# Attention masks as VectorE instructions, two full-width products in place of three, and a scan whose VectorE and ScalarE work stands in program order

## The chip, the cores and the metric

The kernel runs on one core of a Trainium2 chip. The metric is the time of one execution on the device in microseconds (us). TensorE (PE in the profile; PEld is its queue of weight loads) multiplies matrices into PSUM, VectorE (DVE) and ScalarE (ACT) read PSUM and SBUF, GpSimd (POOL) works on SBUF alone, and SyncE (SP) issues the DMAs. Engines wait for one another through semaphores. Each engine takes its own instructions in the order in which the program lists them.

## The reference

One layer of a hybrid encoder over 1024 positions and 1024 channels, all in float32. Three mixers run side by side on the same projection, then they are gated, added, projected, and a gated feed-forward with a short convolution follows. What the change touches is the softmax of the two attentions and the scan:

```python
def blocked_attention(q, k, v, bias_mask):
    ...
    s = jnp.einsum('bqhd,bkhd->bhqk', q_blk, k).astype(jnp.float32) * scale
    p = jax.nn.softmax(bias_mask(i, s), axis=-1).astype(v.dtype)
    return jnp.einsum('bhqk,bkhd->bqhd', p, v)

# first attention:  allowed = (k_idx // 64) <= (q_idx // 64)
# second attention: s = s + Fq - F[k];  allowed = k_idx <= q_idx

def ssd_scan(x, dt, A, Bm, Cm):                 # 16 heads of 64, 2 groups, state 128
    ...
    y_diag = jnp.einsum('bcijg,bcijgh,bcjghp->bcighp', cb, decay, xdt)
    states = jnp.einsum('bcjgn,bcjgh,bcjghp->bcghpn', Bc, decay_to_end, xdt)
    # h[c+1] = h[c] * chunk_decay + states[c]
    y_off = jnp.einsum('bcign,bcghpn,bcigh->bcighp', Cc, h_in, jnp.exp(a_cum))
    return y_diag + y_off
```

Each attention has 8 heads. The scan's result is multiplied by a gate and normed over its 1024 channels.

## The kernel before

The positions are cut into eight tiles of 128. Products are made of a high and a low half of each operand (names ending in h and l), so that a product of two float32 matrices is three TensorE passes. The stages follow each other: norm and projections (to about 410 us), the two attentions (about 418 to 925 us), the scan (about 925 to 1120 us), the three branch projections, the output projection, and the feed-forward.

**Attention** is 64 units: 16 heads (8 of the first attention, then 8 of the second), each with four units `jp` of two query tiles. For each query tile `score_row` makes the scores, in one chunk of up to 512 keys or in two, in a PSUM tile of the ring `a_s` (3 buffers). The mask of the last 128 keys is added by TensorE too: a product of a bfloat16 unit matrix `identb` with a constant mask (`mmla` for the first attention, `mfox` for the second) into the same PSUM tile (L955). VectorE takes the row's maximum of each chunk (L957; L964 where there are two), ScalarE the exponential (L967), VectorE the reciprocal of the sum (L973), GpSimd multiplies (L974). Two units later `values` transposes the probabilities 128 by 128 on TensorE (L1021), ScalarE copies them out as the high half `pth` (L1026), VectorE makes the low half `ptl` (L1027), and `pv` multiplies by the values (L992 to L1000). The stationary operand of `pv` is `o.vv`, 128 columns wide: 64 columns of high half, 64 of low half. For the last key tile of a unit, which concerns only one of the two query tiles, three products with 64 of these columns each are made (L997 to L999). All products of a unit add up in one half of the PSUM tile `o_acc`; `done` copies its two partition halves with ScalarE into `o1` and `o2` (L1005, L1006; two buffers each), VectorE adds them (L1009) and SyncE stores the sum in `att_d` (L1010).

**The scan** is eight chunks `c`, each in three parts that run one step apart: `ssd_a` (transposes of x, the decay matrices E), `ssd_b` (products with E, products with the state, the next state, the gate and the norm's root), `ssd_c` (transposes of the result, store in `ys_d`).

**Order.** In both stages TensorE also works on the projections of gates and convolution inputs, the fill (`all_fill`, L862): 36 blocks of 48 products, of 512 columns each. `merge` interleaves the streams of a step by planned costs (`cost_s`, `cost_v`, the numbers in `yield`), and the fill gets a share by the sum of the costs. The work of the other engines is put in a list with a planned time (`later`), and issued when the planned clock has come there; `force` issues early what TensorE's next instruction needs. `tc.manual_schedule` names the engines whose instructions stay in that written order: TensorE and VectorE in attention, TensorE alone in the scan. The order on the other engines is made by a scheduler when the program is built.

Of the kernel before, what the change touches and what calls it, by code (L numbers as in the profile page):

```python
# [21 lines left out]
P = 128  # L22
# [20 lines left out]
def block_kernel(ctx: ExitStack, tc: tile.TileContext, x, positions, norm_mix_g, w_in, b_gate,  # L43
# [51 lines left out]
    identb = const([P, P], BF16, "identb")  # L95
    G.tensor_copy(identb, ident)
# [12 lines left out]
    mmla = const([P, P], BF16, "mmla")  # L109
    G.memset(mmla, 0.0)  # L110
    G.memset(mmla[0:64, 64:128], NEG)
# [826 lines left out]
    def score_row(o, i, pn):  # L938
        mask = (mmla, mfox)[o.br]
# [7 lines left out]
        for ci, (a, b) in enumerate(chunks):  # L947
# [3 lines left out]
            for i_, (q_, k_) in enumerate(o.passes):  # L951
                T.matmul(ps[:, :w], q_[:, qs], k_[:, a:a + w], start=i_ == 0,  # L952
                         stop=not last and i_ == len(o.passes) - 1)
            if last:
                T.matmul(ps[:, b - a - P:b - a], identb, mask, start=False, stop=True)  # L955
            c = len(o.passes) * w / 2400
            later(c + 0.1, lambda ps=ps, ci=ci, a=a, b=b: V.reduce_max(  # L957
# [20 lines left out]
        yield c + 0.05  # L978
# [6 lines left out]
    def values(o, jp, pn):  # L985
# [3 lines left out]
        def pv(kp, th, tl):  # L989
# [3 lines left out]
            if full:  # L993
                T.matmul(po, o.vv[:, k1, :], th[:, 256:512], start=False, stop=False)
                T.matmul(po, o.vv[:, k1, :], tl[:, 256:512], start=False, stop=False)
            else:
                T.matmul(po[0:64, 128:256], o.vv[:, k1, 0:64], th[:, 256:384], start=False, stop=False)  # L997
                T.matmul(po[0:64, 128:256], o.vv[:, k1, 64:128], th[:, 256:384], start=False, stop=False)
                T.matmul(po[0:64, 128:256], o.vv[:, k1, 0:64], tl[:, 256:384], start=False, stop=False)  # L999
# [48 lines left out]
    def cost_s(jp, n=3):  # L1048
        return sum(n * max(b - a, 256) / 2400 for i in (2 * jp, 2 * jp + 1) for a, b in row_chunks(i)) + 0.1
# [6 lines left out]
    with ExitStack() as pt__:  # L1056
# [7 lines left out]
        a_o2 = Ring(atp, [64, 256], F32, "o2", 2)  # L1064
# [33 lines left out]
    with ExitStack() as ps__:  # L1098
# [36 lines left out]

        def ssd_a(o, c):

            if c + 1 < NT:
                seg_rows(c + 1)
                load_bc(obj[c + 1], c + 1)  # L1140
            xT = pool.tile([P, D], F32, name=uid("xT"), tag="xT", bufs=1)
            for g in range(2):
                pt = psp.tile([P, 512], F32, name=uid("stp"), tag="ts", bufs=2)
                for j in range(4):
                    T.transpose(pt[:, j * P:j * P + P], o.xs[:, 4 * g + j, :], ident)
                A.activation(xT[:, 512 * g:512 * g + 512], pt, AF.Copy)
                yield 0.44
# [4 lines left out]
            V.tensor_mul(o.xdt, xv, hb(dt, c))  # L1152
            o.xdd = pool.tile([P, 16, 64], F32, name=uid("xdd"), tag="xdd", bufs=1)
            V.tensor_mul(o.xdd, xv, hb(dend, c))
            o.y = pool.tile([P, 16, 64], F32, name=uid("y"), tag="y", bufs=3)
            V.tensor_mul(o.y, xv, Db.unsqueeze(2).to_broadcast([P, 16, 64]))
            o.E = []
            o.bT = pool.tile([P, 2, P], F32, name=uid("bT"), tag="bT")
            for g in range(2):
                hs = slice(8 * g, 8 * g + 8)  # L1160
                pcb = psp.tile([P, 512], F32, name=uid("pcb"), tag="seg", bufs=2)
                T.matmul(pcb[:, 0:P], o.bc[:, g, :], o.bc[:, 2 + g, :], start=True, stop=True)
                cbm = pool.tile([P, P], F32, name=uid("cbm"), tag="cbm")
                T.transpose(pcb[:, P:2 * P], o.bc[:, g, :], ident)
                V.tensor_mul(cbm, pcb[:, 0:P], tri)
                A.activation(o.bT[:, g, :], pcb[:, P:2 * P], AF.Copy)
                yield 0.33
                for q in range(2):
                    pse = psp.tile([P, 512], F32, name=uid("pse"), tag="seg", bufs=2)
# [5 lines left out]
                    A.activation(E, pse.rearrange("p (h i) -> p h i", h=4), AF.Relu, scale=-1.0)  # L1175
                    A.activation(E, E, AF.Exp, scale=-1.0)
                    V.tensor_mul(E, E, cbm.unsqueeze(1).to_broadcast([P, 4, P]))
# [3 lines left out]
        def ssd_b(o, c, prev):  # L1181

            zt, _ = f_t4.get()
            SY.dma_start(zt, z_d[c * P:c * P + P, :])
            for g in range(2):
                hs = slice(8 * g, 8 * g + 8)
                py = psp.tile([P, 8, 64], F32, name=uid("py"), tag="py", bufs=2)
                for q in range(2):
                    for hh in range(4):
# [4 lines left out]
                V.tensor_add(o.y[:, hs, :], o.y[:, hs, :], py)  # L1194
                yield 0.88
                if prev is not None:
                    po = psp.tile([P, 512], F32, name=uid("pof"), tag="ts", bufs=2)
                    T.matmul(po, o.bc[:, 2 + g, :], prev.hst[:, hs, :], start=True, stop=True)
                    tmp = pool.tile([P, 8, 64], F32, name=uid("yo"), tag="yo", bufs=1)
                    V.tensor_mul(tmp, po.rearrange("p (h d) -> p h d", d=64), hb(ea, c, hs))  # L1200
                    V.tensor_add(o.y[:, hs, :], o.y[:, hs, :], tmp)
                    yield 0.86
            if c + 1 < NT:
                o.hst = pool.tile([P, 16, 64], F32, name=uid("hst"), tag="hst")
                for g in range(2):
                    hs = slice(8 * g, 8 * g + 8)
                    ps_ = psp.tile([P, 512], F32, name=uid("pst"), tag="ts", bufs=2)
                    T.matmul(ps_, o.bT[:, g, :], o.xdd[:, hs, :], start=True, stop=True)
                    psv = ps_.rearrange("p (h d) -> p h d", d=64)
                    if prev is None:  # L1210
                        V.tensor_copy(o.hst[:, hs, :], psv)
                    else:
                        V.tensor_mul(o.hst[:, hs, :], prev.hst[:, hs, :], hb(cdec, c, hs))
                        V.tensor_add(o.hst[:, hs, :], o.hst[:, hs, :], psv)
                    yield 0.86
            yf = o.y.rearrange("p h d -> p (h d)")
            V.scalar_tensor_tensor(out=yf, in0=yf, scalar=0.5, in1=zt, op0=ALU.mult, op1=ALU.mult)
            o.yT = pool.tile([P, 8, P], F32, name=uid("yT"), tag="yT", bufs=1)
            ss = pool.tile([P, 1], F32, name=uid("yss"), tag="yss")
            A.activation(o.yT.rearrange("p j s -> p (j s)"), yf, AF.Square, accum_out=ss)  # L1220
# [552 lines left out]
```

## Time and the profile before

| what | value |
|---|---|
| time of three runs | 2058.81, 2062.83, 2064.87 us, median 2062.83 us |
| the profiled execution | 2061.22 us; its span (first to last instruction) 2059.5 us |
| busy: PE, DVE, ACT, POOL | 98%, 67%, 46%, 30% of the span |
| mean granted clock of TensorE | 0.993 of full speed |
| attention, 418 to 925 us | DVE about 70% busy, ACT about 60% |
| scan, 925 to 1120 us | DVE about 70% busy, ACT about 50% |

In the timeline a row is one instruction, or several equal ones that follow each other (x3): when it started, how long it took, engine, line and operation, the tile written and the tiles read by the program's names (qk, pth, ptl, o, s, mm), then partitions and columns, and in brackets how long the engine had been idle and who ended that. The ends of matmuls are modelled, so the distance from one start to the next, the pitch, says what an instruction cost TensorE. Groups of instructions have a row with the count, the busy time, the mean duration of one in ns, and the idle time ahead of them with what ended it.

### The profile page before, as it was taken

How to read it: one execution, taken by the hardware profiler on the slowest of the kernel's cores; microseconds unless marked ns; L12 is line 12 of the kernel's file. 1: busy time of each engine (PE TensorE's matmuls, PEld its weight loads, DVE VectorE, ACT ScalarE, POOL GpSimd, SP SyncE). 2: the span in 40 equal slices, each digit the busy share in tenths (PEclk: the TensorE clock that was granted, in tenths of full speed). 3: DMA queues.
4: the chain of work that ended last, by engine and by line, in shares of the span. 5: the costliest groups of instructions: out<-in, count | busy, mean ns of one | idle time of the engine just before them, and what ended most of it. 6: DMA issues, size and time to landing. Idle time of an engine off the chain costs nothing.

```text
span 2059.5 us, 28796 instructions
## 1 busy us (share of the span) xinstructions
PE 2009.7 (98%) x10233; PEld 1685.1 (82%) x10233; DVE 1388.7 (67%) x2498; ACT 940.5 (46%) x1722; POOL 611.0 (30%) x604
## 2 busy tenths in 40 slices
PE   7999899999999999999999999999899999999999
PEld 7899678888888888888778888888688888878887
DVE  7678479366667766755774455567987787775655
ACT  5555323156556666555553222223544454444432
POOL 4345233222222222210000040001654445412655
PEclk9999999999999999999999999999999999999999
DMA  5158767655344455324432664431322322329665
GB/s 168 45 169 263 256 221 243 197 155 142 109 123 112 133 134 133 101 83 146 139 121 95 230 215 145 156 130 52 92 82 72 102 72 73 101 94 350 216 230 195
DMA packets 274792, 303.60 MB, mean 147 GB/s; under 512 B 18860, under 2 KB 206520, under 8 KB 274648
## 3 DMA queue, kind: packets, MB, share of 16 engines
q1 hardware_dynamic: 274648, 301.76, 46.7%
q8 instruction: 81, 1.33, 0.3%
q14 instruction: 63, 0.52, 0.1%
HBM read 209.03 MB, written 92.67 MB: 146 GB/s over the span
## 4 chain that ended last, share of the span: by engine, by line
PE 81%; DVE 9%; DMA 4%; ACT 2%; issue 2%; POOL 1%; SPq 1%; ACTq 0%; DVEq 0%; POOLq 0%
PE mm L862 19%; PE ybr L163 8%; PE dn L1720 8%; PE ua L1388 5%; PE ud L1388 5%; PE uc L1388 5%; PE fx L163 4%; PE wo L1434 4%; PE s L952 4%; PE tp L1021 3%; PE ub L1388 2%; PE fxv L163 2%; PE q L163 1%; PE py L1190 1%; PE kv L163 1%
## 5 line engine op out<-in xcount | busy, mean ns | idle before, releaser
L862 PE MATMUL mm<-hnh,wh 128*128 128x512 f32 x576 | 247.3, 429 | 0.0
L862 PE MATMUL mm<-hnh,wl 128*128 128x512 f32 x576 | 226.6, 393 | 0.0
L862 PE MATMUL mm<-hnl,wh 128*128 128x512 f32 x576 | 225.2, 391 | 0.0
L974 POOL TENSOR_SCALAR pm<-pm,rs 128x128 f32<-128x128 f32 (+7 forms) x128 | 107.9, 845 | 347.9 <-DVE rs L973 313.8
L1720 PE MATMUL dn<-dr,dr 128*128 128x512 f32 x592 | 182.1, 389 | 0.0
L1027 DVE TENSOR_TENSOR ptl<-tp,pth 128x512 fp32r<-128x512 f32 (+1 forms) x160 | 101.3, 633 | 83.0 <-ACT pth L1026 81.9
L957 DVE TENSOR_REDUCE nmx<-s 128x1 f32<-128x128 f32 (+2 forms) x192 | 105.7, 551 | 57.4 <-PE s L955 45.7
L967 ACT ACTIVATE pm<-s,nmx 128x128 f32<-128x128 f32 (+2 forms) x192 | 109.6, 575 | 55.6 <-DVE nmx L964 38.1
L1720 PEld LDWEIGHTS dn<-dr,dr 128*128 128x128 f32 x592 | 111.1, 188 | 23.0
L862 PEld LDWEIGHTS mm<-hnh,wl 128*128 128x128 f32 x576 | 108.1, 188 | 24.9
L862 PEld LDWEIGHTS mm<-hnh,wh 128*128 128x128 f32 x576 | 108.8, 189 | 17.9 <-issue 4.1
L862 PEld LDWEIGHTS mm<-hnl,wh 128*128 128x128 f32 x576 | 109.0, 189 | 17.6 <-issue 3.1
L1026 ACT ACTIVATE pth<-tp 128x512 fp32r<-128x512 f32 (+1 forms) x160 | 88.2, 551 | 70.1 <-PE tp L1021 69.3
L952 PE MATMUL s<-qk,qk 96*128 96x384 f32 (+5 forms) x480 | 117.8, 350 | 0.9 <-ACT pm L967 0.9
L1720 PE MATMUL dn<-dr 128*128 128x512 f32 x296 | 115.3, 389 | 0.4 <-DVE dY L1737 0.4
L1299 POOL TENSOR_TENSOR mg<-mg,gl 128x512 f32<-128x512 f32 x16 | 24.9, 1559 | 299.1 <-DVE gl L1296 297.6
L139 DVE TENSOR_TENSOR dr<-dr,dr 128x1024 fp32r<-128x1024 f32 x52 | 72.2, 1388 | 55.6 <-ACT dr L138 53.2
L163 PE MATMUL fx<-w5h,hnh 128*128 128x512 f32 x256 | 103.2, 403 | 2.1 <-ACT w5h L138 2.1
L163 PE MATMUL fx<-w5l,hnh 128*128 128x512 f32 x256 | 101.4, 396 | 1.4 <-DVE w5l L139 1.4
L163 PE MATMUL fx<-w5h,hnl 128*128 128x512 f32 x256 | 101.1, 395 | 0.0
L163 PE MATMUL ybr<-al,wh 128*128 128x512 f32 x256 | 99.2, 389 | 0.0
L163 PE MATMUL ybr<-ah,wl 128*128 128x512 f32 x256 | 98.3, 389 | 0.0
(492 smaller groups left out, 5698.3 us busy)
## 6 DMA issues: line engine op xcount, KB each, us to landing
dr<-act_d SPq DMA_DIRECT2D x99, 256.0 KB
wr<-in_ffn_w_up_dram SPq DMA_DIRECT2D x47, 512.0 KB
wr<-in_w_in_dram SPq DMA_DIRECT2D x36, 512.0 KB
g_d<-t SPq DMA_DIRECT2D x24, 512.0 KB
gl<-g_d SPq DMA_DIRECT2D x24, 512.0 KB
ws<-in_ffn_w_down_dram SPq DMA_DIRECT2D x22, 512.0 KB
wsum_d<-ws SPq DMA_DIRECT2D x22, 512.0 KB
act_d<-fa SPq DMA_DIRECT2D x22, 512.0 KB
```

The lines of the kernel that those rows point to most:

```text
L139: return i, le.tensor_sub(l, src, f32(h))
L163: T.matmul(ps, a(k), b(k), start=(i == 0), stop=(i == n - 1))
L862: T.matmul(ps, a[:, k, :], b[half][:, k, :], start=(k == 0 and i == 0), stop=(k == NK - 1 and i == 2))
L952: T.matmul(ps[:, :w], q_[:, qs], k_[:, a:a + w], start=i_ == 0, stop=not last and i_ == len(o.passes) - 1)
L957: later(c + 0.1, lambda ps=ps, ci=ci, a=a, b=b: V.reduce_max(nmx[:, ci:ci + 1], ps[:, :b - a], axis=AX, negate=True))
L967: pss[ci][1][0] = later(c + 0.9 + 0.1 * ci, lambda ci=ci, a=a, b=b: A.activation(p_[:, a:b], pss[ci][0][:, :b - a], AF.Exp, bias=nb, accum ...
L974: G.tensor_scalar(p_[:, 0:n * P], p_[:, 0:n * P], rs[:, 3:4], 0.0, op0=ALU.mult, op1=ALU.add)
L1026: later(c + 0.05, lambda th=th, pt=pt, off=off: A.activation(th[:, :off], pt[:, :off], AF.Copy))
L1027: pl[0] = later(c + 0.6, lambda th=th, tl=tl, pt=pt, off=off: V.tensor_sub(tl[:, :off], pt[:, :off], f32(th[:, :off])))
L1388: T.matmul(ps, a, b, start=first and n == 0, stop=n == 11, skip_group_check=not first)
L1434: T.matmul(p, a, b, start=k == 0 and i == 0, stop=k == NK - 1 and i == 2)
L1720: T.matmul(ps[m], a[:, ts_], b[:, 512:], start=first_ and j == 0 and q == 0, stop=j == NFH - 1 and q == 2, skip_group_check=not first_)
```

## The change

The TensorE products that added the masks are gone, with the constants `identb` and `mmla`. In their place VectorE writes the last 64 keys of the first 64 queries with the mask's value (`memset`, first attention), or adds `mfox` to the last 128 keys (`tensor_add`, second attention), ahead of the row's maximum. In `pv` the three products with 64 columns become two with all 128 (the high half of the probabilities, then the low half; the second adds a term of low times low). `o2` has six buffers. Two planned costs lose the mask's share. In the scan VectorE and ScalarE keep program order as well; their instructions get planned times by `later`, PSUM tiles come from rings (`s_ts`, `s_seg`, `s_py`, two buffers each as before), and `xdd`, `yT`, `yo` and `cbm` have twice the buffers.

```diff
-    identb = const([P, P], BF16, "identb")
-    G.tensor_copy(identb, ident)
...
-    mmla = const([P, P], BF16, "mmla")
...
     def score_row(o, i, pn):
...
                 T.matmul(ps[:, :w], q_[:, qs], k_[:, a:a + w], start=i_ == 0,
-                         stop=not last and i_ == len(o.passes) - 1)
-            if last:
-                T.matmul(ps[:, b - a - P:b - a], identb, mask, start=False, stop=True)
+                         stop=i_ == len(o.passes) - 1)
             c = len(o.passes) * w / 2400
-            later(c + 0.1, lambda ps=ps, ci=ci, a=a, b=b: V.reduce_max(
+            if last and o.br == 0:
+                later(c + 0.1, lambda ps=ps, e=b - a: V.memset(ps[0:64, e - 64:e], NEG))
+            elif last:
+                later(c + 0.1, lambda d=ps[:, b - a - P:b - a]: V.tensor_add(d, d, mfox))
+            later(c + 0.101, lambda ps=ps, ci=ci, a=a, b=b: V.reduce_max(
...
-        yield c + 0.05
+        yield c
...
-                T.matmul(po[0:64, 128:256], o.vv[:, k1, 0:64], th[:, 256:384], start=False, stop=False)
-                T.matmul(po[0:64, 128:256], o.vv[:, k1, 64:128], th[:, 256:384], start=False, stop=False)
-                T.matmul(po[0:64, 128:256], o.vv[:, k1, 0:64], tl[:, 256:384], start=False, stop=False)
+                T.matmul(po[:, 128:256], o.vv[:, k1, :], th[:, 256:384], start=False, stop=False)
+                T.matmul(po[:, 128:256], o.vv[:, k1, :], tl[:, 256:384], start=False, stop=False)
...
-        return sum(n * max(b - a, 256) / 2400 for i in (2 * jp, 2 * jp + 1) for a, b in row_chunks(i)) + 0.1
+        return sum(n * max(b - a, 256) / 2400 for i in (2 * jp, 2 * jp + 1) for a, b in row_chunks(i))
...
-        a_o2 = Ring(atp, [64, 256], F32, "o2", 2)
+        a_o2 = Ring(atp, [64, 256], F32, "o2", 6)
...
         def ssd_a(o, c):
...
-            V.tensor_mul(o.xdt, xv, hb(dt, c))
...
+            o.rdt = later(1.3, lambda: V.tensor_mul(o.xdt, xv, hb(dt, c)))
+            later(2.6, lambda: V.tensor_mul(o.y, xv, Db.unsqueeze(2).to_broadcast([P, 16, 64])))
+            o.rdd = xT_read[0] = later(3.9, lambda: V.tensor_mul(o.xdd, xv, hb(dend, c)))
...
         def ssd_b(o, c, prev):
...
-            A.activation(o.yT.rearrange("p j s -> p (j s)"), yf, AF.Square, accum_out=ss)
...
+            later(3.1, lambda: A.activation(o.yT.rearrange("p j s -> p (j s)"), yf, AF.Square, accum_out=ss))
+            later(4.3, root)
+            o.ry = later(6.3, lambda: A.activation(yf, yf, AF.Copy, scale=r))
...
-        with tc.manual_schedule(engines={mybir.EngineType.PE}):
+        with tc.manual_schedule(engines={mybir.EngineType.PE, mybir.EngineType.DVE, mybir.EngineType.Activation}):
```

The order on TensorE, at the seam between the second and the third unit of a head of the first attention. The rows are in program order: line, operation, tile written and tiles read, columns. Before (s: scores, o: the values' sum, tp: transposes, mm: fill):

```order
L952 MATMUL s_5744<-qk_1143_5285,qk_1146_5288 128x256
L955 LDWEIGHTS identb
L955 MATMUL s_5744<-mmla,identb 128x128
L992 MATMUL o<-pth_5648,vv_5189 128x256
L997 MATMUL o<-pth_5648,vv_5189 64x128
L998 MATMUL o<-pth_5648,vv_5189 64x128
L999 MATMUL o<-ptl_5649,vv_5189 64x128
L1000 MATMUL o<-ptl_5649,vv_5189 128x256
L1021 MATMUL tp_5760<-ident,pm_5508 128x128
L1021 MATMUL tp_5760<-ident,pm_5538 128x128 x2
L862 MATMUL mm_5766<-hnh_124,wh_5345 128x512
```

Of the fill six products (L862) follow here, and then the third unit's first L992. In the changed program, at the same seam:

```order
L946 MATMUL s_5734<-qk_1151_5278,qk_1154_5281 128x256
L988 MATMUL o<-pth_5639,vv_5183 128x256
L993 MATMUL o<-pth_5639,vv_5183 128x128
L994 MATMUL o<-ptl_5640,vv_5183 128x128
L995 MATMUL o<-ptl_5640,vv_5183 128x256
L1016 MATMUL tp_5749<-ident,pm_5501 128x128
L1016 MATMUL tp_5749<-ident,pm_5528 128x128 x2
L988 MATMUL o<-pth_5691,vv_5183 128x256
```

The mask's pair of rows is gone, three narrow products are two wide ones, and here the fill has moved to another place, so that only three transposes stand between the second unit's last product and the third's first. Over the whole stage eight of the 63 seams had only three transposes before, and nine have now; the fill has 29 products fewer in attention and 30 more behind the scan.

On VectorE, at the same row of the second attention, before (nmx: maxima, ptl: low half):

```order
L957 TENSOR_REDUCE nmx_8204<-s_8206 128x1
L1027 TENSOR_TENSOR ptl_8215<-tp_8210,pth_8214 128x384
L957 TENSOR_REDUCE nmx_8204<-s_8225 128x1
L964 TENSOR_TENSOR nmx_8204<-nmx_8204 128x1
L957 TENSOR_REDUCE nmx_8231<-s_8233 128x1
```

and in the changed program:

```order
L953 TENSOR_REDUCE nmx_8142<-s_8144 128x1
L1022 TENSOR_TENSOR ptl_8153<-tp_8148,pth_8152 128x384
L952 TENSOR_TENSOR s_8169<-s_8169,mfox 128x128
L953 TENSOR_REDUCE nmx_8142<-s_8169 128x1
L960 TENSOR_TENSOR nmx_8142<-nmx_8142 128x1
L953 TENSOR_REDUCE nmx_8184<-s_8186 128x1
```

One instruction has come in ahead of the last maximum of each row.

On VectorE in the scan, from the root of one chunk's norm to the first mask product of the next chunk's decay (cbm), before (yr: root, xdt, y, xdd: products with x, wl: fill, py: PSUM of ssd_b):

```order
L155 SCALAR_TENSOR_TENSOR yr_3959_11930<-rs_t_11936,yr_3959_11930 128x1
L1152 TENSOR_TENSOR xdt_12004<-xT_11950,dt 128x1024
L1156 TENSOR_TENSOR y_12008<-xT_11950,Db 128x1024
L151 SCALAR_TENSOR_TENSOR rs_t_11939<-yr_3959_11930,rs_v_11934 128x1
L155 SCALAR_TENSOR_TENSOR yr_3959_11930<-rs_t_11939,yr_3959_11930 128x1
L151 SCALAR_TENSOR_TENSOR rs_t_11942<-yr_3959_11930,rs_v_11934 128x1
L155 SCALAR_TENSOR_TENSOR yr_3959_11930<-rs_t_11942,yr_3959_11930 128x1
L1194 TENSOR_TENSOR y_11798<-y_11798,py_11984 128x512
L811 TENSOR_TENSOR wl_12025<-wr_12022,wh_12024 128x1024
L1165 TENSOR_TENSOR cbm_12013<-pcb_12011,tri 128x128
```

and in the changed program:

```order
L146 SCALAR_TENSOR_TENSOR rs_t_11880<-yr_4199_11814,rs_v_11872 128x1
L150 SCALAR_TENSOR_TENSOR yr_4199_11814<-rs_t_11880,yr_4199_11814 128x1
L1154 TENSOR_TENSOR xdt_11857<-xT_11819,dt 128x1024
L1155 TENSOR_TENSOR y_11859<-xT_11819,Db 128x1024
L1156 TENSOR_TENSOR xdd_11858<-xT_11819,dend 128x1024
L806 TENSOR_TENSOR wl_11838<-wr_11835,wh_11837 128x1024
L1200 TENSOR_TENSOR y_11657<-y_11657,py_11886 128x512
L1165 TENSOR_TENSOR cbm_11909<-seg_11907,tri 128x128
```

The root is no longer spread between other work: it stands in one piece, and xdd, which stood behind the state's sums, has moved ahead of wl.

More of the change, by code (lines that the diff above doesn't have):

```diff
@@ L1134, in hb @@
             return t[:, c, hs].unsqueeze(2).to_broadcast([P, hs.stop - hs.start, 64])
+        s_ts, s_seg, s_py = (Ring(psp, [P, 512], F32, n, 2) for n in ("ts", "seg", "py"))
+        xT_read = [None]
         def ssd_a(o, c):
@@ L1215, in ssd_b @@
+                        pl[0] = later(1.0, lambda hs=hs, psv=psv: V.tensor_add(
+                            o.hst[:, hs, :], o.hst[:, hs, :], psv))
+                    o.rh.append(pl[0])
                     yield 0.86
             yf = o.y.rearrange("p h d -> p (h d)")
-            V.scalar_tensor_tensor(out=yf, in0=yf, scalar=0.5, in1=zt, op0=ALU.mult, op1=ALU.mult)
-            o.yT = pool.tile([P, 8, P], F32, name=uid("yT"), tag="yT", bufs=1)
+            o.yT = pool.tile([P, 8, P], F32, name=uid("yT"), tag="yT")
@@ L1227, in ssd_c @@
+            zl[0] = later(1.8, lambda: V.scalar_tensor_tensor(out=yf, in0=yf, scalar=0.5, in1=zt,
+                                                              op0=ALU.mult, op1=ALU.mult))
+            later(3.1, lambda: A.activation(o.yT.rearrange("p j s -> p (j s)"), yf, AF.Square, accum_out=ss))
+            later(4.3, root)
+            o.ry = later(6.3, lambda: A.activation(yf, yf, AF.Copy, scale=r))
         def ssd_c(o, c):
+            force(o.ry)
             yf = o.y.rearrange("p h d -> p (h d)")
@@ L1230, in ssd_c @@
             for g in range(2):
[L1231 removed]
+                pt, pl = s_ts.get()
                 for j in range(4):
                     T.transpose(pt[:, j * P:j * P + P], yf[:, (4 * g + j) * P:(4 * g + j + 1) * P], ident)
[L1234 removed]
+                pl[0] = later(0.54, lambda g=g, pt=pt: A.activation(
+                    o.yT[:, 4 * g:4 * g + 4, :], pt.rearrange("p (j s) -> p j s", j=4), AF.Copy))
@@ L1235, in ssd_c @@
+                if g == 1:
+                    o.out = later(1.2, lambda: SY.dma_start(
+                        ys_d[:, :, c * P:c * P + P].rearrange("j p s -> p j s"), o.yT))
                 yield 0.44
-            SY.dma_start(ys_d[:, :, c * P:c * P + P].rearrange("j p s -> p j s"), o.yT)
-        with tc.manual_schedule(engines={mybir.EngineType.PE}):
+        with tc.manual_schedule(engines={mybir.EngineType.PE, mybir.EngineType.DVE, mybir.EngineType.Activation}):
             obj = {c: Head() for c in range(NT)}
@@ L1257, in block_kernel @@
                     break
+            force(obj[NT - 1].out)
     mix.close()
```

77 lines of the change are left out of this document (41 added, 36 removed).

## The prediction

> **What bounds the kernel now.** First the page's top and its chain that ended last.
>
> ```profile
> span 2059.5 us, 28796 instructions
> PE 81%; DVE 9%; DMA 4%; ACT 2%; issue 2%; POOL 1%; SPq 1%; ACTq 0%; DVEq 0%; POOLq 0%
> ```
>
> Four fifths of the chain are TensorE. Then the view of busy time by windows, for the stages that change: two windows of attention (PE, PEld, DVE, ACT, POOL busy us and instructions, granted clock, DMA share, GB/s), one of the scan.
>
> ```profile
> 600.00:700.00 100.00, 98.79 (x601) 84.03 (x600) 69.07 (x158) 61.27 (x156) 25.38 (x29) 1.00 0.48 130
> 700.00:800.00 100.00, 99.38 (x604) 84.13 (x603) 73.75 (x165) 64.47 (x158) 24.85 (x29) 1.00 0.49 129
> 950.00:1050.00 100.00, 99.39 (x531) 79.53 (x531) 71.83 (x133) 51.53 (x90) 0.00 (x0) 1.00 0.42 126
> ```
>
> TensorE is busy for 99 us of 100 at full clock, VectorE for about 70. Busy need not mean needed, so I read who TensorE waits for, in the view of waits over the whole run (us in total, times, longest):
>
> ```profile
> PE o L992 <- ACT o L1006: 8.2, 11, 1.5
> PE s L952 <- ACT pm L967: 0.9, 2, 0.6
> PE stp L1145 <- DVE rs_v L147: 0.4, 1, 0.4
> ```
>
> In attention it waits for the copy of the values' sum, and almost never for VectorE's part of the softmax; in the scan it waits 0.4 us in all. So in both stages **a TensorE instruction saved is time saved**, and a faster order in the scan has nothing to give. A change to VectorE counts only where it becomes late for TensorE.
>
> **Term 1, the 128 mask products.** TensorE's timeline, by pitch: a mask with a product of the values behind it, and the same products without a mask ahead.
>
> ```profile
> 560.06 0.23 PE L955 MATMUL s<-mmla,identb 128*128 128x128 bf16 x1
> 560.10 0.36 PE L992 MATMUL o<-pth,vv 128*128 128x256 f32 x1
> 560.30 0.22 PE L997 MATMUL o<-pth,vv 128*64 128x128 f32 x1
> ...
> 565.28 0.28 PE L992 MATMUL o<-pth,vv 128*128 128x256 f32 x1
> 565.40 0.22 PE L997 MATMUL o<-pth,vv 128*64 128x128 f32 x1
> ```
>
> The mask has a pitch of 0.04 us, and L992 behind it one of 0.20, against 0.12 without. So this mask costs 0.04 + 0.08 = 0.12 us, though its own pitch looks like nothing. Behind other masks stand transposes:
>
> ```profile
> 573.85 0.23 PE L955 MATMUL s<-mmla,identb 128*128 128x128 bf16 x1
> 573.92 0.60 PE L1021 MATMUL tp<-ident,pm 128*128 128x128 f32 x4
> 574.28 0.48 PE L862 MATMUL mm<-hnh,wh 128*128 128x512 f32 x1
> ...
> 568.86 0.60 PE L1021 MATMUL tp<-ident,pm 128*128 128x128 f32 x4
> 569.21 0.47 PE L862 MATMUL mm<-hnh,wh 128*128 128x512 f32 x1
> ```
>
> Here the mask costs 0.07, and the four transposes 0.36 instead of 0.35: 0.08 in all. In the order of instructions before, 84 masks have a product behind them and 44 have transposes: 84 x 0.12 + 44 x 0.08 = **13.6 us** saved.
>
> **Term 2, three narrow products become two wide ones.** A pitch of 0.06 for each of L997 to L999 would promise 64 x 0.06 = 3.8 us. But the last product behind them is not free:
>
> ```profile
> 565.29 0.14 PEld L997 LDWEIGHTS o<-pth,vv 128*64 128x64 f32 x1
> ...
> 565.52 0.19 PEld L1000 LDWEIGHTS o<-ptl,vv 128*128 128x128 f32 x1
> ...
> 560.48 0.33 PE L1000 MATMUL o<-ptl,vv 128*128 128x256 f32 x1
> 560.65 0.39 PE L862 MATMUL mm<-hnh,wh 128*128 128x512 f32 x1
> 560.88 0.40 PE L862 MATMUL mm<-hnl,wh 128*128 128x512 f32 x1
> ...
> 568.62 0.29 PE L995 MATMUL o<-ptl,vv 128*128 128x256 f32 x1
> 568.74 0.28 PE L1000 MATMUL o<-ptl,vv 128*128 128x256 f32 x1
> ```
>
> L1000 behind the narrow products has a pitch of 0.17, while behind L995 it has 0.12 (568.74 to 568.86, quoted above). The load of 128 columns takes 0.19, that of 64 columns 0.14: 64 columns more are 0.05 more, so 128 columns need about 0.11 of the load path. Under a narrow product of 0.06 that load doesn't hide, and 0.05 is left over. Products of few columns under full loads show the same bound:
>
> ```profile
> 1036.43 1.89 PE L1190 MATMUL py<-xdt,E 128*128 128x64 f32 x16
> 1038.16 0.44 PE L1162 MATMUL pcb<-bc 128*128 128x128 f32 x2
> ```
>
> Sixteen in 1.73 us are 0.11 each. Now the two wide products: each streams 128 columns (0.06) while the next full load (0.11) runs, so each has a pitch of 0.11. Before: 0.12 + 3 x 0.06 + 0.17 = 0.47. Changed: 0.12 + 2 x 0.11 + 0.12 = 0.46. I take 64 x 0.01 = **0.6 us** saved; the ends are 3.8 saved (both wide ones at 0.06, the one behind them still at 0.17) and 2.6 lost (0.11 each, with L1000 staying at 0.17: 0.51, 64 x 0.04).
>
> [...]
>
> **Term 3, six output copies.** Most waits for L1006 look like this one: a unit ends, three transposes, and the next unit's first product finds the sum not yet copied out.
>
> ```profile
> 571.47 0.34 PE L1000 MATMUL o<-ptl,vv 128*128 128x256 f32 x1
> 571.65 0.49 PE L1021 MATMUL tp<-ident,pm 128*128 128x128 f32 x3
> 572.74 0.39 PE L992 MATMUL o<-pth,vv 128*128 128x256 f32 x1 [0.60 <-ACT o L1006]
> ...
> 857.11 0.38 ACT L1006 ACTIVATE o<-o 64x256 f32<-64x256 f32 x1 [2.59 <-DMA att_d<-o]
> ACT o L1006 <- DMA att_d<-o: 4.6, 3, 2.6
> ```
>
> From 571.65, three transposes should have ended 0.24 later (0.35 for four above, less 0.11), at 571.89: 0.85 us lost. This has nothing to do with `o2`; it belongs to seams with three transposes alone, eight before and nine now: **0.9 us lost**. What six buffers remove is ScalarE's wait for the store, 4.6 us in three places. The longest, 2.6 us, held TensorE for up to 1.5 (its longest wait, above). I take **3 us** saved, between 1.5 and 4.6.
>
> **Term 4, VectorE's new work in attention.** 64 times a `memset` of 64 x 64 and 64 times an addition of 128 x 128 in PSUM. The second isn't in the trace; nearest are the products with `tri` from PSUM, and for the first the one larger `memset` on VectorE:
>
> ```profile
> L1165 DVE TENSOR_TENSOR cbm<-pcb,tri 128x128 f32<-128x128 f32 x16 | 4.5, 283 | 1.1 <-PE pcb L1164 1.1
> L651 DVE MEMSET neg<- x1: 165/165/165, 283.5 to 283.5; 8x128 f32 x1
> ```
>
> At 0.28 and at most 0.17 us, VectorE gets 18 us more in the second attention (about 240 us long: from some 72% busy to 80%) and 11 in the first. It isn't the bound, so the question is whether a row's chain gets late. TensorE may fill a score buffer again when ScalarE has read the chunk three before it. A typical one of the second attention:
>
> ```profile
> 714.19 0.58 ACT L967 ACTIVATE pm<-s,nmx 128x384 f32<-128x384 f32 x1 [0.18 <-DVE rs L972]
> ...
> 715.49 0.51 PE L952 MATMUL s<-qk,qk 128*128 128x384 f32 x2
> ```
>
> The buffer is free at 714.77, and wanted at 715.49: 0.72 us to spare. Of the 189 such distances five are under 0.2 us, four from 0.37 to 0.48, and the rest 0.66 or more. A chain longer by 0.28 makes TensorE wait where less was to spare, about 1 us in all, if a queue forms once or twice. I take **1 us** lost, from 0 to 6 (25 tight buffers late by 0.25 each).
>
> **Term 5, the scan in program order.** 0.4 us of wait is all there is to gain. To lose, VectorE must be late for the decay products, which reuse PSUM behind `cbm`.
>
> ```profile
> 1027.10 1.22 DVE L1217 SCALAR_TENSOR_TENSOR y<-y,t 128x1024 f32<-128x1024 f32 x1
> 1031.37 1.06 ACT L1220 ACTIVATE yT<-y 128x1024 f32<-128x1024 f32 x1 [1.58 <-DMA ys_d<-yT]
> 1032.56 0.15 DVE L1222 TENSOR_SCALAR yv<-yss 128x1 f32<-128x1 f32 x1 [1.99 <-ACT yT L1220]
> L1177 DVE TENSOR_TENSOR E<-E,cbm 128x512 f32<-128x512 f32 x32 | 22.0, 687 | 14.0 <-ACT E L1176 14.0
> ```
>
> In the new order VectorE has, from the state's last sum to `cbm`: the sum and an E (0.69 each), the gate (1.22), the wait for the square (1.06 and a read, 1.2), the root (ten small ones of 0.15 or a little more, 1.7), xdt, y, xdd and wl (1.22 each, as wide as the gate), one PSUM sum (0.69), `cbm` (0.28): 11.4 us. TensorE meanwhile has 30 fill products (0.23 each by the rows of L862 above, 6.9), three groups of four L1190 (0.86 each, 2.6), eight transposes (0.9), and pof, pst, pcb and two decay products, some 2.5: 12.9 us. VectorE is 1.5 us ahead, so **0**, from 0.4 gained to 8 lost (1 us in each chunk). Two buffers for yT also take away the wait of 1.58 for the store, which cost TensorE nothing.
>
> The fill's 29 products that leave attention come back behind the scan, where TensorE is the bound too: 0.
>
> **Sum.** 13.6 + 0.6 - 0.9 + 3 - 1 = 15.3 us saved. The profiled execution took 2061.22 us, 1.7 more than its span: 2045.9, and its like against the median of 2062.83, which is 1.6 above it, 2047.5. I say **2046 us**.
>
> **Rivals.**
> - *The mask's replacement is late.* For it: each row's chain grows by up to 0.28 us on an engine that stands at 70%. Against: 0.66 us or more to spare in 180 of 189 places. Price 6 us at the tight buffers: 2052.
> - *The scan stalls, and the kernel is slower.* The root now stands in one piece and waits for ScalarE's square with xdt, xdd, wl and `cbm` queued behind it; `cbm` is waited for by ScalarE's copy, and that by TensorE. It decides once the square comes over 1.5 us later than I count; for a kernel slower than before, each of eight chunks must lose 2 us and more, so the square be 3.5 us late: 2046 + 8 x 2.7 = 2068. For it: the wait of 1.99 above. Against: part of it was the store's. [...] No run so far shows this order.
> - *The wide products are cheap.* If they had the pitch of 0.06, 3.2 us more are saved: 2043. For it: that is what L997 to L999 show. Against: the 0.11 of L1190.
> - *Masks cost their own pitch only.* If the longer product behind a mask had another cause, 128 x 0.05 = 6.4 us are saved in place of 13.6: 2053. Against: 0.20 and 0.12 for the same L992.
>
> **How the numbers follow.** Forecast 62%, with 2041 to 2051 for its own; late masks 14%; scan 6%; wide products 10%; masks for their own pitch 8%. The range goes from 2039 (all upper ends of terms 2 and 3 together: 2046 - 3.2 - 1.6, and 2 for the spread of runs) to 2056 (late masks, with half of what the scan can lose). Runs differ by about 0.3%, which is what can be told from no change: 6.2 us, so faster means under 2056.6. The forecast and the wide products lie under it (72%), own pitch mostly (6 of 8), late masks half (7 of 14): 85% faster; within 0.3% 11%; slower 4%, from the scan.
>
> **What would show it.** The first value product (L992 before) at a pitch of 0.12 wherever scores stand ahead; the two wide products at 0.11, and the one behind at 0.12; no ScalarE wait for att_d; nine waits of 0.85 for L1001; waits of scores for exponentials of about 2 us in all; in the scan under 1 us of TensorE waits. A wait of TensorE for ScalarE's copy beside `cbm`, chunk after chunk, would make me wrong, and so would scores that wait in each unit of the second attention.

## The result and the profile after

The changed kernel takes 2048.31 us in the median of five runs (2043.96 to 2050.93), the kernel before 2062.82 beside it (2058.25 to 2064.87): a ratio of 0.9939, with a 95% interval from 0.9924 to 0.9955, or 14.5 us less by the medians, 12.6 by the ratio, 9.3 to 15.7 by the interval. The profiled execution took 2043.96 us. Its page has this span and this chain:

```profile
span 2042.2 us, 28558 instructions
PE 84%; DVE 9%; DMA 2%; ACT 2%; issue 2%; POOL 1%; SPq 1%; ACTq 0%; DVEq 0%; POOLq 0%
```

and its view of waits these rows for TensorE in attention and in the scan (us in total, times, longest):

```profile
PE o L988 <- ACT o L1001: 7.3, 11, 1.2
PE tp L1016 <- POOL pm L970: 0.9, 1, 0.9
PE tp L1016 <- DVE ptl L1022: 0.9, 2, 0.7
PE seg L1171 <- ACT bT L1166: 0.6, 1, 0.6
PE s L946 <- ACT pm L963: 0.4, 2, 0.2
```

The scan waits once, for ScalarE's copy beside `cbm`. In attention the waits for the output copy are as many as before (11), with 7.3 us in place of 8.2, and transposes now wait too.

Spans don't say where the time went, so I measure two stretches by TensorE's timeline, each without its fill (0.231 us a product). **Attention** goes from the first product of the scores to the scan's first transposition: 253.2 us before (511.0 less 1116 products), 244.0 after (494.9 less 1086). **The scan** goes from there to near the end of the first branch projection behind it: 253.1 and 251.6. So the change is worth 9.2 + 1.5 = 10.7 us in what it touches. The other 6.6 of the two profiled executions lie ahead of attention (4.8) and far behind the scan (1.8), in code that is the same. The view by windows shows why, ahead of attention; the kernel before first:

```profile
80.00:100.00 20.00, 16.64 (x87) 15.61 (x85) 12.20 (x44) 9.54 (x33) 2.12 (x10) 0.83 0.37 115
280.00:300.00 20.00, 17.77 (x80) 14.54 (x79) 16.79 (x50) 6.63 (x13) 5.10 (x4) 0.91 0.60 169
```

and the changed kernel:

```profile
80.00:100.00 20.00, 15.34 (x96) 14.28 (x96) 13.36 (x47) 10.11 (x34) 2.10 (x10) 1.00 0.38 115
280.00:300.00 20.00, 20.00 (x97) 16.58 (x96) 18.08 (x57) 6.88 (x11) 5.12 (x4) 1.00 0.73 217
```

The number behind POOL's busy time is the granted clock: 0.83 and 0.91 in one, 1.00 in the other. The clock differs between executions of one kernel too: the means of the changed kernel's five runs go from 0.992 to 0.996. Runs of the kernel before, 61 of them in the comparisons below, go from 2055.75 to 2067.32. Single differences under some 4 us are therefore read from the stretches, not from the times.

TensorE's pitches behind scores, where a mask stood before, in the changed kernel's timeline:

```profile
555.73 0.86 PE L946 MATMUL s<-qk,qk 96*128 96x512 f32 x3
556.43 0.28 PE L988 MATMUL o<-pth,vv 128*128 128x256 f32 x1
556.55 0.22 PE L993 MATMUL o<-pth,vv 128*128 128x128 f32 x1
556.61 0.28 PE L994 MATMUL o<-ptl,vv 128*128 128x128 f32 x1
556.73 0.33 PE L995 MATMUL o<-ptl,vv 128*128 128x256 f32 x1
556.89 0.52 PE L946 MATMUL s<-qk,qk 96*128 96x256 f32 x3
```

L988 has 0.12, as forecast; the wide products have 0.06 and 0.12, the one behind them 0.16. Together 0.46, as forecast, though otherwise shared out.

Now a place that came out worse. The first score product of the seventh query tile's second chunk waits for the exponential of the sixth tile's first chunk, which frees its buffer. ScalarE there in the kernel before, and TensorE:

```profile
461.63 0.58 ACT L967 ACTIVATE pm<-s,nmx 128x384 f32<-128x384 f32 x1 [2.10 <-DVE nmx L964]
462.20 0.57 ACT L967 ACTIVATE pm<-s,nmx 128x384 f32<-128x384 f32 x1
462.76 0.59 ACT L1026 ACTIVATE pth<-tp 128x512 fp32r<-128x512 f32 x1
...
462.93 0.39 PE L862 MATMUL mm<-hnh,wl 128*128 128x512 f32 x1
463.16 0.69 PE L952 MATMUL s<-qk,qk 96*128 96x384 f32 x3
463.69 0.23 PE L955 MATMUL s<-mmla,identb 128*128 128x128 bf16 x1
```

and in the changed kernel, with VectorE's minimum on which the exponential rests:

```profile
457.36 0.16 DVE L960 TENSOR_TENSOR nmx<-nmx 128x1 f32<-128x1 f32 x1
...
457.77 0.60 ACT L1021 ACTIVATE pth<-tp 128x512 fp32r<-128x512 f32 x1 [2.13 <-PE tp L1016]
458.26 0.58 ACT L963 ACTIVATE pm<-s,nmx 128x384 f32<-128x384 f32 x1
458.82 0.58 ACT L963 ACTIVATE pm<-s,nmx 128x384 f32<-128x384 f32 x1
...
458.67 0.40 PE L857 MATMUL mm<-hnh,wl 128*128 128x512 f32 x1
458.98 0.80 PE L946 MATMUL s<-qk,qk 96*128 96x384 f32 x3
459.62 0.28 PE L988 MATMUL o<-pth,vv 128*128 128x256 f32 x1
```

The minimum is there at 457.52, but ScalarE's next instruction is now the copy `pth`, which starts at 457.77, and the exponential comes at 458.26. TensorE's pitches show the rest: the last fill product takes 0.31 in place of 0.23, the three score products 0.64 in place of 0.53. That is 0.19 us, without a wait in the rows of TensorE's matmuls, since the modelled end of the last fill product (458.67 + 0.40 = 459.07) lies behind the start of the scores (458.98). The queue of weight loads does show one, of 0.34 us:

```profile
458.98 0.47 PEld L946 LDWEIGHTS s<-qk,qk 96*128 96x128 f32 x3 [0.34 <-ACT pm L963]
```

In ScalarE's program order `pth` stands ahead of this exponential in 16 heads of 16; before it stood there in 3. Before, those three heads and no others showed the longer pitches; now all do.

By pitch (what each instruction's distance to the next exceeds that of its kind where nothing is waited for), TensorE loses 18.5 us in attention now, 13.4 before: 10.1 ahead of the values' products (11.3 before), 5.5 at scores (2.0), 2.8 at transposes (none).

### The profile page after: what moved, and what is told of

It is laid out like the page before. It is cut to its first block, busy times and chain, and to the rows that moved or that the text cites. A ratio compares the mean times of both kernels' runs of the same rounds, so it can differ in the third digit from the quotient of the medians.

```text
span 2042.2 us, 28558 instructions
## 1 busy us (share of the span) xinstructions
PE 1991.4 (98%) x10041; PEld 1678.7 (82%) x10041; DVE 1410.3 (69%) x2626; ACT 944.5 (46%) x1722; POOL 617.3 (30%) x601
## 4 chain that ended last, share of the span: by engine, by line
PE 84%; DVE 9%; DMA 2%; ACT 2%; issue 2%; POOL 1%; SPq 1%; ACTq 0%; DVEq 0%; POOLq 0%
PE mm L857 18%; PE dn L1743 10%; PE ybr L158 9%; PE fx L158 6%; PE ua L1411 5%; PE uc L1411 5%; PE ud L1411 5%; PE wo L1457 4%; PE s L946 4%; PE tp L1016 3%; PE ub L1411 3%; PE fxv L158 1%; PE py L1196 1%; PE kv L158 1%; PE q L158 1%
## 5 line engine op out<-in xcount | busy, mean ns | idle before, releaser
L970 POOL TENSOR_SCALAR pm<-pm,rs 128x128 f32<-128x128 f32 (+7 forms) x128 | 113.1, 886 | 327.7 <-DVE rs L969 199.9
L963 ACT ACTIVATE pm<-s,nmx 128x128 f32<-128x128 f32 (+2 forms) x192 | 109.8, 578 | 37.3 <-DVE nmx L960 24.4
```

The costliest lines, as they stand in the source:

```text
L963: pss[ci][1][0] = later(c + 0.9 + 0.1 * ci, lambda ci=ci, a=a, b=b: A.activation(p_[:, a:b], pss[ci][0][:, :b - a], AF.Exp, bias=nb, accum ...
L970: G.tensor_scalar(p_[:, 0:n * P], p_[:, 0:n * P], rs[:, 3:4], 0.0, op0=ALU.mult, op1=ALU.add)
```

## The experiments

All runs in one table. Time is the median with the interval of the ratio to the kernel before (a median of 2060.8 to 2061.6 in each of the three sets of runs, and of 2062.8 beside the changed kernel); the stretches are as above; waits are TensorE's in attention by pitch.

| kernel | time, us | ratio's interval | attention | waits | scan |
|---|---|---|---|---|---|
| before | 2060.8 to 2061.6 | | 253.2 | 13.4 | 253.1 |
| changed | 2048.3 | 0.9924 to 0.9955 | 244.0 | 18.5 | 251.6 |
| masks only | 2060.7 | 0.9990 to 1.0017 | 260.1 | 34.0 | 252.3 |
| no mask | 2044.5 | 0.9900 to 0.9936 | 238.8 | 13.8 | 251.6 |
| ScalarE's order | 2053.7 | 0.9956 to 0.9980 | 249.6 | 23.8 | 251.7 |
| seams | 2046.5 | 0.9914 to 0.9959 | 244.6 | 18.8 | 251.6 |
| two o2 | 2060.5 | 0.9979 to 1.0005 | 255.2 | 29.3 | 251.7 |
| scan only | 2060.4 | 0.9980 to 1.0008 | 256.3 | 16.6 | 252.5 |
| seams, fill from behind | 2046.4 | 0.9899 to 0.9951 | 237.2 | 11.7 | 255.7 |
| more fill | 2050.8 | 0.9930 to 0.9968 | 242.6 | 17.3 | 256.4 |
| six o2 only | 2055.8 | 0.9962 to 0.9988 | 251.6 | 11.8 | 252.9 |
| seams, half and half | 2041.6 | 0.9898 to 0.9930 | 240.8 | 15.2 | 251.8 |
| mask twice | 2055.6 | 0.9960 to 0.9987 | 252.1 | 26.2 | 252.0 |
| narrow | 2046.4 (one run) | | 243.3 | 17.6 | 251.6 |

Some of these traces have stretches in which TensorE was granted half its clock. How long they are follows from the mean clock of windows around them: 4.00 us at 0.57 in two o2 (from 846 us) are 3.4 us at half and the rest at full clock; 2.70 at 0.79, 2.00 at 0.50 and 2.00 at 0.93 in masks only (from 726.3 us) are 3.4 as well; the 6.8 us in ScalarE's order below are twice that. A stretch of 3.4 us is so worth up to 1.7 us. The columns include them. I count, in attention, three in masks only, two in ScalarE's order, one each in seams, two o2, more fill and mask twice, and in the scan's stretch one in more fill; the windows are shown for two o2, for ScalarE's order and for one of masks only, not for the others. The kernel before and the changed one have none there: their clock is 1.00 in each window of 50 us from 450 to 1150 us.

**Masks only**, on the kernel before:

```diff
-                T.matmul(ps[:, b - a - P:b - a], identb, mask, start=False, stop=True)
+            if last and o.br == 0:
+                later(c + 0.1, lambda ps=ps, e=b - a: V.memset(ps[0:64, e - 64:e], NEG))
+            elif last:
+                later(c + 0.1, lambda d=ps[:, b - a - P:b - a]: V.tensor_add(d, d, mfox))
```

> The kernel before with the masks on VectorE alone (and the planned costs that go with them): three narrow value products, two o2 buffers and the old scan stay. Theory A (as forecast: the 128 products are worth 13.6 us and VectorE's work costs 1): about 12.6 us under the kernel before, 2050. Theory B (ScalarE's order: in this program, as in the changed one, the copy pth stands ahead of the exponential of the sixth query tile's first chunk in 16 of 16 heads, in the kernel before in 3; the scores that reuse its buffer wait 0.1 to 0.2 us in each head, and a few single waits come with it, 5 us in all): about 8.5 us under, 2054, with 16 scores of a pitch 0.1 too long.

Neither: nothing is gained. TensorE's work fell by the 12.4 us of the masks in attention (228.3 to 215.9 without waits and fill), but its waits rose by 20.6. The views of waits of this kernel, of TensorE and of ScalarE:

```profile
PE o L993 <- ACT o L1007: 17.4, 14, 4.1
ACT o L1007 <- DMA att_d<-o: 16.4, 7, 3.8
```

The largest part is the output copy, and behind it the store: by pitch some 10 of the 20.6 us. Another 5 are by my count the three stretches at half the clock, which follow waits of 2.1, 2.1 and 4.1 us for that copy (the clock is shown for the first alone), and some 6 stand at scores and transposes, as in the changed kernel. That made the next theory, the one of the pair (masks and buffers bring a gain only together), and the run with two o2 buffers.

**No mask**, on the changed kernel:

```diff
-            if last and o.br == 0:
-                later(c + 0.1, lambda ps=ps, e=b - a: V.memset(ps[0:64, e - 64:e], NEG))
-            elif last:
-                later(c + 0.1, lambda d=ps[:, b - a - P:b - a]: V.tensor_add(d, d, mfox))
```

> The changed kernel without any mask, on TensorE or on VectorE: the scores of forbidden keys stay in, nothing else is left out. In its program pth stands ahead of that exponential in 2 of 16 heads, so the two theories agree here on a gain: if VectorE's masks with all that follows cost 5 us, 2043; if they cost the 1 us of the forecast, 2047. The scores' extra pitch of 0.1 in each head goes by both.

Attention is 5.2 us shorter than in the changed kernel: this is what the masks on VectorE cost, five times the forecast. Waits at scores fall from 5.5 to 2.1, at transposes from 2.8 to 1.1. The two heads with `pth` ahead are the only ones in which the longer pitches are left.

**ScalarE's order**, on the changed kernel:

```diff
-        with tc.manual_schedule(engines={mybir.EngineType.PE, mybir.EngineType.DVE}):
+        with tc.manual_schedule(engines={mybir.EngineType.PE, mybir.EngineType.DVE, mybir.EngineType.Activation}):
```

> The changed kernel with ScalarE in program order in attention too; VectorE's masks stay as they are. pth then stands ahead of the sixth tile's first exponential in 0 of 16 heads (between its two exponentials in 7). Theory A' (VectorE's own time, 0.11 to 0.29 us more in the chain, makes the scores late): the extra pitches stay, 2048. Theory B (ScalarE's order): they go, 16 x 0.19 = 3 us less, 2045. Against both: copies of the fill in program order may stand in the way of other exponentials, then it gets slower than 2048 and new waits show.

Slower by 5, and still the place in question tells the theories apart. ScalarE and TensorE there:

```profile
459.22 0.58 ACT L963 ACTIVATE pm<-s,nmx 128x384 f32<-128x384 f32 x1 [2.04 <-DVE nmx L960]
459.80 0.57 ACT L963 ACTIVATE pm<-s,nmx 128x384 f32<-128x384 f32 x1
460.35 0.59 ACT L1021 ACTIVATE pth<-tp 128x512 fp32r<-128x512 f32 x1
...
460.15 0.39 PE L857 MATMUL mm<-hnh,wl 128*128 128x512 f32 x1
460.38 0.69 PE L946 MATMUL s<-qk,qk 96*128 96x384 f32 x3
460.91 0.28 PE L988 MATMUL o<-pth,vv 128*128 128x256 f32 x1
```

0.23 and 0.53 again, with VectorE's mask still in the chain; so in all eight heads of the first attention, and in six of the second. The regular 0.19 us (3.0 in 16 heads) is ScalarE's order. What it lost stands elsewhere: program order makes copies stand behind exponentials whose maximum isn't there yet. The worst place, ScalarE and then TensorE:

```profile
836.07 0.47 ACT L963 ACTIVATE pm<-s,nmx 128x256 f32<-128x256 f32 x1 [2.14 <-DVE nmx L953]
837.17 0.38 ACT L1000 ACTIVATE o<-o 64x256 f32<-64x256 f32 x1
...
838.01 0.58 PE L988 MATMUL o<-pth,vv 128*128 128x256 f32 x1 [3.42 <-ACT o L1001]
```

TensorE's clock is halved from 836.3 to 843.1, and the 5.1 us of this behind the wait cost another 2.5. Both ends are worked out from the view by windows (granted clock third from the end), with half or full clock in each window:

```profile
834.00:838.00 4.00, 0.55 (x3) 0.31 (x3) 2.69 (x6) 1.89 (x6) 1.56 (x3) 0.79 0.95 177
838.00:840.00 2.00, 1.99 (x8) 1.90 (x9) 0.65 (x2) 0.85 (x2) 0.00 (x0) 0.50 0.39 119
840.00:843.00 3.00, 3.00 (x10) 2.50 (x9) 2.64 (x7) 1.16 (x3) 0.03 (x1) 0.50 0.33 85
843.00:846.00 3.00, 3.00 (x20) 2.66 (x19) 1.09 (x2) 1.00 (x2) 0.85 (x1) 0.98 0.50 195
```

So this one place accounts for most of the 5.6 us that attention is longer.

**Seams**, on the changed kernel (`o_at` is the planned time of the last unit's end):

```diff
         if kp == 0:
             force(o_last[jp % 2])
+            if clk[0] - o_at[0] < 1.6:
+                owed[0] -= advance(fill) or 0.0
```

> The changed kernel with six products of the fill put ahead of a unit's first product of the values wherever less than 1.6 us are planned since the last unit's end. The eleven waits for the output copy, 7.3 us by the view of waits and 10 us by pitch, should go: 8 to 10 us less, 2039. If the waits are a debt that TensorE pays elsewhere (fill spent here is missing in another place, where scores then wait), the gain is under 4 us.

The waits for the output copy go from 10.1 to 0.1 by pitch, and the scores' rise from 5.5 to 14.5: a debt, and with the stretch at half the clock that I count behind a score's wait of 1.6 us (the clock there is not shown) it is paid in full (18.5 us of waits before, 18.8 now).

**Two o2 buffers**, on the changed kernel:

```diff
-        a_o2 = Ring(atp, [64, 256], F32, "o2", 6)
+        a_o2 = Ring(atp, [64, 256], F32, "o2", 2)
```

> The changed kernel with two o2 buffers, as before the change. By the forecast, six buffers are worth 3 us (1.5 to 4.6): 2051, 2053 at most. By the theory that came out of masks alone (where ScalarE waited 16.4 us for the stores and TensorE 17.4 us for ScalarE's output copies, so that nothing was left of the masks' 13.6 us): the buffers are worth 9 to 13 us in this kernel, 2058 to 2061, with seven or so waits of ScalarE for att_d, and TensorE's waits for the output copy at 15 to 18 us in place of 7.3.

As by the theory of the pair: 12 us by the times, 11.2 by the stretch of attention. The view of waits, for TensorE and ScalarE:

```profile
PE o L988 <- ACT o L1001: 16.7, 14, 3.8
ACT o L1001 <- DMA att_d<-o: 16.0, 8, 3.5
```

and SyncE's queue in the timeline, ahead of the longest of these waits:

```profile
834.58 0.99 SPq L919 DMA_DIRECT2D qk<-fk_h  x2
835.62 0.46 SPq L919 DMA_DIRECT2D qk<-fk_l  x1
836.18 0.55 SPq L1005 DMA_DIRECT2D att_d<-o  x1
836.78 1.23 SPq L919 DMA_DIRECT2D qk<-fq_h  x2
838.05 0.51 SPq L919 DMA_DIRECT2D qk<-fq_l  x1
838.65 0.40 SPq L802 DMA_DIRECT2D wr<-in_w_in_dram  x1
840.21 5.20 SPq L1005 DMA_DIRECT2D att_d<-o  x1
```

The six loads of the next head and a weight block go out first; the store behind them, which else takes 0.45 us to issue (the median of 64), takes 5.20. With six buffers such a store is as slow (4.46 in the changed kernel), and nobody waits for it.

**Scan only**, the change's scan on the kernel before.

> The kernel before with the new scan alone. By the forecast 0 (from 0.4 gained to 8 lost). By the traces, where the scan from its first transposition to the fill's last part became 1.2 us shorter: 1 us less, 2060 against 2061; neither can be told from the kernel before by the time, the length of the stage in the trace decides: the scan's part takes 1 to 1.5 us less by theory, and attention the same as before.

The scan's stretch is 0.6 us shorter, half of what was expected. Attention, whose program is the same as before, took 3.1 us more in this execution, with 8.7 us of ScalarE's waits for the store in place of 4.6: with two buffers this loss also varies.

**Seams, with fill from behind the scan**: the line of the run on seams without `owed[0] -=`.

> The changed kernel with the fill put ahead of a unit's first product where less than 1.6 us are planned since the last unit's end, as in the run on the seams, but without taking it from the fill's share of that stretch: it comes from the 66 products behind the scan. If the waits at the seams only moved on because the fill was missing a little later (theory D, debt), now 7 to 10 us are gained: 2039. If the chain from scores to exponentials sets the pace of those units, whatever stands between (theory C), the waits appear at the scores again: 2046 to 2048.

Theory D for attention: 6.8 us shorter, though part of the waits has again moved on to the scores. But the 66 products behind the scan were not spare. Without them the first branch waits for its operand; TensorE from 1110 to 1180 us, where the changed kernel waits for nothing:

```profile
PE ybr L158 <- ACT ah L133: 2.1, 1, 2.1
PE ybr L158 <- DVE al L134: 0.5, 1, 0.5
```

and the scan's stretch is 4.1 longer.

**More fill**: `FILL_ATT = 1.06` in place of 1.0.

> The changed kernel with 6% more fill in attention (66 products more there, 60 fewer behind the scan). TensorE then comes later to each score, by 0.06 of a unit's work, 0.3 us between a score and the one that reuses its buffer. If the late scores come from a chain a little too long (theory D), most of the 5.5 us of score waits and part of the seams go: 4 to 6 us less, 2043. If not, 2048.

Attention gains 1.4, the scan's stretch loses 4.8, again for lack of fill behind it: the first branch waits 2.0 us for its operand, and by my count it then runs 3.4 us at half the clock, 1.7 of the 4.8 (the clock there is not shown). More fill spread evenly doesn't go where it is needed: seven waits of about 0.85 at seams stay.

**Six o2 buffers only**, on the kernel before.

> The kernel before with six o2 buffers alone; masks, products and the scan stay, and so does ScalarE's order. By the forecast 3 us less (1.5 to 4.6): 2058 against 2061. By the theory of the pair (the buffers are worth 11 us where the masks have left TensorE, because the units then follow each other faster than the stores drain, and little where they have not): 1 to 4 us less, so the same here; the two are told apart together with masks alone and with the changed kernel with two buffers. In the trace ScalarE's wait for att_d is 0 and the waits at seams of three transposes stay, about 0.85 each.

5.6 us less by the time (2.5 to 7.8 by the interval), 1.6 by the stretch. So six buffers are worth 5.6 by the times where the masks are on TensorE and 12.2 (2060.5 to 2048.3) where they aren't; by the stretches of attention 1.6 and 11.2. The masks, with the small rest of the change, are worth nothing with two buffers and 7.5 with six. Why times and stretches differ isn't shown. The profiled execution of the kernel before may have been a mild one in attention: scan only, with the same program there, took 3.1 more.

**Seams, half and half**: `owed[0] -= 0.5 * (advance(fill) or 0.0)`.

> The changed kernel with fill at the seams, half of it taken from the fill's share and half from the products behind the scan (24 fewer there, 42 left). If the stretch behind the scan needs about 40 of them to cover its stores and loads (the kernel before has 36 there and waits for nothing), 4 to 6 us less than the changed kernel: 2043. If the debt is paid at the scores as when the whole was taken from the share, 2047.

2041.64 us (2041.16 to 2044.21), under both kernels, though its interval just touches that of the changed kernel. Attention is 3.2 us shorter than in the changed kernel, the scan 0.2 longer. The waits for the copy are down to 0.1, those at scores are 11.0 and at transposes 4.0: part of the debt is still paid there.

**Mask twice**: each of the two VectorE instructions is issued a second time.

> The changed kernel with each mask instruction on VectorE done twice: 0.11 us more in each row's chain in the first attention, 0.29 in the second. ScalarE's order stays (pth ahead in 16 of 16). If VectorE's own time is the price of the masks (theory A'), the second one costs as much as the first, 5 us: 2053. If the price is mostly ScalarE's order (theory B), the second one costs only its own length where a score waits already: 16 to 24 places by 0.1 to 0.3 us, 2 to 4 us: 2051.

8.0 us more in attention, more than theory A' wanted, and some 6.5 without the one stretch at half the clock that I count near a transpose's wait of 1.6 us (the clock there is not shown). But not at the regular place: in the first attention the two pitches there stay at 0.31 and 0.64, where by my estimate `pth` covers another 0.11; in the second the 0.31 becomes 0.34. The rise is at single scores and at transposes that wait for `ptl` (waits at scores 9.6, at transposes 6.1). So both theories hold a part. Of the 5.2 us that the masks cost, ScalarE's order at the regular place is 2.7 (14 heads by 0.19). That the rest is VectorE's own time fits this run but isn't shown: ScalarE's order differs elsewhere too between the changed kernel and the one without masks, and no run keeps the masks and swaps only that copy and that exponential.

**Narrow**: the three products of 64 columns on the changed kernel.

> The changed kernel with the three products of 64 columns again. Load path (theory: a group is bound by its loads and streams together): the group's pitches sum to 0.46 us as with two wide ones, 0.3 us more in all, not seen in the time. Rival of the forecast (wide ones cheap): 3 us more.

TensorE's work in attention without waits is 215.5 in place of 215.1: the wide products save 0.3 us.

## Why the prediction was right, and where it wasn't

The time lies in the range, 2 us above the 2046 forecast, and the sign is right. The terms are less good than the sum: two of them missed, both to the worse, and that the time came so near is partly luck.

- **Term 1 and 2, 14.2 us: right.** TensorE's work without waits fell from 228.3 to 215.1, and fill behind masks by 1.1 more: 14.3. The 0.08 on a mask's successor was real; the rival that counted a mask's own pitch only, falls. So does the rival of cheap wide products: one of the two has 0.06, but the group has the 0.46 that was counted.
- **Term 3: right in kind, wrong in form.** Waits for the copy fell by 1.2 us between the two traces, not by 2.1: eleven stalled seams with 10.1 us, not nine with 7.7. The step that failed took the buffers' worth from the trace of before as if it stood by itself. It depends on term 1: with the masks off TensorE and two buffers, by my count five stores took 2.5 us or more to issue in SyncE's queue (up to 5.20 in two o2), where before one did (2.78), and the gain was gone (masks only, two o2). Whether the shorter units bring the stores to the head's loads, or the order in which SyncE's instructions were put, wasn't told apart. The masks alone don't decide it: the three kernels with more fill in attention (fill from behind, more fill, half and half) have them on VectorE too, and by my count one such store each.
- **Term 4, "I take 1 us lost": the step that failed.** It is 5.2 us. The step counted only VectorE's 0.28 against 0.66 to spare. The durations were right:

```profile
L952 DVE TENSOR_TENSOR s<-s,mfox 128x128 f32<-128x128 f32 x64 | 18.8, 294 | 16.3 <-PE s L946 15.9
L950 DVE MEMSET s<- 64x64 f32 x64 | 7.2, 112 | 25.5 <-PE s L946 24.8 <-ACT t L862 0.3
```

  0.29 and 0.11. Left out was that ScalarE's order is made when the program is built, and turned with them: a copy of 0.6 us went ahead of an exponential in 13 more heads. That exponential then came 0.74 us after its minimum (457.52 to 458.26 above), more than the 0.66 to spare. The rival "the mask's replacement is late" had nearly the price, 6 us, and a seventh of the chance. But its 25 tight buffers don't fit the prediction's own count, which has nine under 0.66, and about half of the 5.2 us came by a way that it didn't name. So its price was near by luck.
- **Term 5, 0:** 0.6 alone and 1.5 in the changed kernel were gained. One wait for `bT` in eight chunks isn't the stall in chunk after chunk that would have made the forecast wrong, so the rival of the stalling scan falls; by how much VectorE is ahead wasn't measured. Beyond the 0.4 us that TensorE's matmuls waited, its weight loads waited 1.3 us for `yo` in three places before (L1208), and nowhere for it now; whether that is the rest of the gain isn't shown. The fill moved behind the scan cost nothing; it may even help there (36 products before, 66 after), since masks only, with the old scan, has 252.3 in place of 253.1.
- **The sum:** 10.7 us in the stretches that the change touches, against 15.3; by the times it is 14.5 in the first runs, and 12.9 against the median of the later 61 of the kernel before. How much of that difference is scatter, in code that is the same, and how much is a mild profiled execution of the kernel before, stays open.

## What to carry to other kernels

An instruction put into a chain can reorder engines that it never touches, where a scheduler makes their order (here `pth` went ahead of an exponential in 16 heads in place of 3): compare the order on every engine of the chain, not only on the one that gets the work. Work taken from the bound engine also moves stores and loads against each other, so a buffer that is worth little before (1.6 us in attention) can carry the whole gain afterwards (11.2); measure such edits as a pair. Fill isn't free to move: where it stands it covers something, and a hole closed in one place opens where the fill was taken (fill from behind: 6.8 us less in attention, 4.1 more in the scan's stretch).

## What the runs showed that I had not expected

**A wait can be followed by a slow clock.** In the kernel with two o2 buffers, TensorE waits 3.8 us, and then fill products have a pitch of 0.43 in place of 0.23. The timeline:

```profile
846.07 0.40 PE L988 MATMUL o<-pth,vv 128*128 128x256 f32 x1 [3.77 <-ACT o L1001]
848.82 0.63 PE L857 MATMUL mm<-hnl,wh 128*128 128x512 f32 x1
849.25 0.61 PE L857 MATMUL mm<-hnh,wl 128*128 128x512 f32 x1
```

and the view by windows over the time behind it (granted clock third from the end):

```profile
846.00:850.00 4.00, 3.93 (x15) 3.50 (x16) 2.38 (x7) 2.52 (x8) 0.48 (x1) 0.57 0.32 101
850.00:853.00 3.00, 3.00 (x21) 2.66 (x19) 1.97 (x5) 0.93 (x2) 0.88 (x1) 1.00 0.45 163
```

With 0.57 of the clock over 4 us, the wait costs about 1.7 us more than its length. In the kernel with masks only the clock fell behind a shorter one too, of 2.1 us, and stayed at 1.00 behind one of 2.0 us that ended at 821.1; the views by windows:

```profile
726.30:729.00 2.70, 2.65 (x17) 2.56 (x18) 2.05 (x5) 1.64 (x4) 0.69 (x1) 0.79 0.03 9
729.00:731.00 2.00, 2.00 (x6) 1.55 (x6) 0.62 (x2) 0.49 (x1) 0.00 (x0) 0.50 0.12 29
731.00:733.00 2.00, 2.00 (x13) 1.83 (x12) 1.11 (x4) 0.13 (x1) 0.00 (x0) 0.93 0.00 0
821.10:824.00 2.90, 2.89 (x18) 2.63 (x19) 1.65 (x4) 1.60 (x4) 0.69 (x1) 1.00 0.14 38
```

In two o2 it stayed at 1.00 behind 2.4 us without a matmul as well:

```profile
756.00:759.00 3.00, 0.58 (x6) 0.35 (x4) 1.02 (x3) 1.48 (x5) 0.00 (x0) 1.00 0.81 310
759.00:762.00 3.00, 3.00 (x19) 2.70 (x20) 1.09 (x3) 1.56 (x4) 0.69 (x1) 1.00 0.34 122
```

So the length of the wait alone doesn't decide it; what else does wasn't found.

**A wait can hide behind a modelled end.** 0.19 us in each of 16 heads stood in no row of TensorE's matmuls in the view of waits; pitches of 0.31 for 0.23 and 0.64 for 0.53 showed it. The waits of the weight loads for these exponentials (L963) rose with it: 8.4 us in 25 places over attention, against 2.6 in 5 before (L967).
